# The down projection of a ConvFFN as seven block products over halves of tokens, channels and columns

## The chip, the cores and the metric

The kernel runs as one program on one core of a Trainium2 chip. The metric is the device time of one execution, in microseconds (us), from the first instruction of the program to its end. The kernel before the change has a median of 1789.0 us over three runs (1784.94 to 1791.03 us). Beside these there is one profiled execution, and the rows in this document come from it.

## The reference

One layer of a decoder step for 1024 prompt tokens and 64 sample tokens that share weights. Only the last part is touched here. After the attention branches the layer adds a ConvFFN, and after that comes the final norm:

```python
def conv_ffn(h, prefix, w_gate, w_up, conv_w, conv_b, w_down):
    L = h.shape[1]
    g = h @ w_gate
    u = h @ w_up
    ...
    f = (jax.nn.gelu(gc) * u) @ w_down
...
    x = x + f
...
y_prompt = rmsnorm(xp, final_norm_g)
```

Everything is float32. The down product is (tokens x 2816) @ (2816 x 1024). The inner width is D_FF = 2816 = 22 blocks of 128 channels.

## The kernel before, in words

A float32 product is made of three TensorE passes: each operand is split into a high part (a cast to fp32r on ACT, line 109) and a low part (source minus high part, on DVE, line 110), and high*high, high*low and low*high are summed in PSUM (`PASSES`, line 172). So every 128x1024 block that enters a product costs one ACT cast and one DVE subtraction. `split` is the helper that issues the two.

Lines 1169 to 1183 make the gate and up products. They run in 22 rounds of seven block products each (`products`), and the product gelu(gate)*up of a round is made on POOL (line 1182) and written to a DRAM tensor `f_d`, as 22 blocks of 128 channels x 1024 tokens (line 1183).

Line 1184 finishes the sample tokens' activations `fsv`: two small transposes on TensorE (`tr`, line 106), a multiply on DVE (line 1057) and the split into `fs` (line 1194).

Lines 1226 to 1266 are the down projection. Token tiles of 128 go in three groups of 3, 3 and 2. A group keeps two PSUM banks for each of its tiles, and walks over the 22 channel blocks: for each block it loads 128x1024 weights (`wr`, 512 KB, split into `wd`), for each pair of blocks the group's activations (`fr`, split into `fh`), and multiplies. A block with three tiles has 18 matmuls of 128x512. The sample tokens ride along in the second group: four matmuls per block (line 1258). The last group holds back its last four blocks and runs them tile by tile. `fin` (line 1203) adds the residual, sums squares on ACT, makes the reciprocal root (`rstd_of`, lines 112 to 123: six small DVE operations and one ACT root), scales on DVE and stores from SP's queue.

The order is that of a scheduler that keeps the program's dependencies and lays every engine's instructions in one row; each engine executes its row in order. All loads of this part are issued by SP, in order too. Raw weights and activations share a ring of four buffers (`raw`), split ones a ring of five (`hl`).

In the code after the change the same names hold. A "step" is one channel block of one block product, that is 12 matmuls (or 14 with the sample); `hd` is its split pair of operands.

Of the kernel before, what the change touches and what calls it, by code (L numbers as in the profile page):

```python
# [16 lines left out]
P = 128  # L17
# [15 lines left out]
def hybrid_step(ctx, tc, x_prompt, x_sample, mem_prompt, cache_k, cache_v, page_table, state_pool,  # L33
# [30 lines left out]
    ps = ctx.enter_context(tc.tile_pool(name="ps", bufs=1, space=bass.MemoryType.PSUM))  # L64
# [13 lines left out]
    def tpb():  # L78
        if tp2[0]:
# [5 lines left out]
    tp2 = [True, 0]  # L85

# [918 lines left out]
    with tc.tile_pool(name="fa", bufs=1, reuse_waits="tile") as fa:  # L1005
# [187 lines left out]
        fs = ap_.tile([P, NF, P], F32R, tag="act", bufs=4, name="fs")  # L1193
        split(fs[:, :, 0:TS], fs[:, :, TS:P], fsv)

    pB_cm.__exit__(None, None, None)
    with tc.tile_pool(name="fb", bufs=1, reuse_waits="tile") as fb:
        fr_b = [fb.tile([P, 2, 384], F32, name=f"fr{i}") for i in range(3)]
        fh_b = [fb.tile([P, 2, 2, 384], F32R, name=f"fh{i}") for i in range(3)]
        gfb = fb.tile([P, D], F32, name="gfb")  # L1200
        nc.sync.dma_start(gfb, bc(final_norm_g, P))

        def fin(t, banks, n, src, dst):
            xt = fb.tile([P, D], F32, tag="y", bufs=4, name=f"y{t}")[:n]
            nc.sync.dma_start(xt, src)
            ss2 = sm.tile([P, 2], F32, tag="ss2", name=f"ss{uid()}")[:n]
            for nb in range(2):
                xh = xt[:, nb * 512:(nb + 1) * 512]
                nc.vector.tensor_tensor(xh, xh, banks[nb][:n], op=ALU.add)
                if n < P:  # L1210
                    nc.vector.tensor_tensor(xh, xh, banks[nb][n:P], op=ALU.add)
                nc.scalar.activation(banks[nb][:n], xh, AF.Square, accum_out=ss2[:, nb:nb + 1])
            ss = sm.tile([P, 1], F32, tag="ss", name=f"ss{uid()}")[:n]
            nc.vector.tensor_tensor(ss, ss2[:, 0:1], ss2[:, 1:2], op=ALU.add)
            r = rstd_of(ss, n, 1.0 / D, 1)
            for nb in range(2):
# [109 lines left out]
```

## Time and profile before

| | |
|---|---|
| median of three runs | 1789.0 us |
| time of the profiled execution | 1788.88 us |
| its span, first to last instruction | 1787.1 us |
| mean granted TensorE clock | 0.987 of full speed |
| TensorE busy | 1724.8 us, 97% |
| DVE, ACT, POOL busy | 893.2, 724.4, 394.8 us |
| mean DMA rate | 131 GB/s |

The profiled execution lies 0.1 us from the median, and 1.8 us of it lie outside the span. A busy TensorE says only that matmuls were in its pipe; how fast they follow each other is read from the starts of groups in the timeline. The granted clock is a share of full speed: 1.00 is 2.4 GHz and 0.50 is 1.2 GHz.

### The profile page before, as it was taken

The page shows a single profiled execution, that of the slowest core. Times are in us where ns is not written, and L with a number is a line of the kernel's source. Part 1 is how long each engine was busy: PE and PEld are TensorE (multiplying, and loading weights), DVE is VectorE, ACT ScalarE, POOL GpSimd, SP SyncE. Part 2 cuts the span into 40 slices and gives each one's busy share as a digit, 9 for nine tenths or more (in the row PEclk, how much of TensorE's full clock was granted, in tenths as well). Part 3 has the DMA queues.
Part 4 walks back from the last instruction along what each step waited for, and adds up shares of the span by engine and source line. Part 5 has one row for each costly group of instructions (what it writes and reads, how often), then busy time and mean ns, then how long its engine had stood idle before and what let it go on. Part 6 is the DMA issues. An engine that isn't in the chain of part 4 may idle for free.

```text
span 1787.1 us, 23047 instructions
## 1 busy us (share of the span) xinstructions
PE 1724.8 (97%) x8289; PEld 1350.8 (76%) x8289; DVE 893.2 (50%) x1576; ACT 724.4 (41%) x1397; POOL 394.8 (22%) x428
## 2 busy tenths in 40 slices
PE   7999999998999999999989899999999999999997
PEld 5887876764666777767767688888888887888886
DVE  6411134230221666676725776666666666444365
ACT  5321235331221666665413344444444444333343
POOL 1113020301100324202201344444444441000000
PEclk9999999999999999999999999999999999999999
DMA  7432251367566334155442132222222224656454
GB/s 279 141 137 74 78 176 54 116 202 248 180 205 194 126 91 132 36 183 159 155 159 77 60 62 75 77 77 78 80 77 77 79 75 144 225 174 215 138 193 150
DMA packets 138600, 234.75 MB, mean 131 GB/s; under 512 B 25823, under 2 KB 71677, under 8 KB 138485
## 3 DMA queue, kind: packets, MB, share of 16 engines
q1 hardware_dynamic: 123349, 187.16, 32.8%
q0 software_dynamic: 15136, 46.12, 7.5%
q8 instruction: 65, 1.06, 0.2%
q14 instruction: 50, 0.41, 0.1%
HBM read 182.74 MB, written 50.54 MB: 131 GB/s over the span
## 4 chain that ended last, share of the span: by engine, by line
PE 86%; DVE 4%; DMA 3%; issue 2%; ACT 2%; SPq 1%; POOL 1%; DVEq 0%; POOLq 0%; ACTq 0%
PE nat L178 18%; PE big L1128 17%; PE big L1223 10%; PE nat L187 8%; PE nat L1128 7%; PE big L178 4%; PE tp L106 3%; PE nat L1223 3%; PE av L1043 3%; PE nat L195 2%; PE av L807 2%; PE big L777 2%; PE av L106 1%; PE av L567 1%; PE big L671 1%
## 5 line engine op out<-in xcount | busy, mean ns | idle before, releaser
L178 PE MATMUL nat<-act,hl 128*128 128x512 f32 x1344 | 359.1, 405 | 0.0
L178 PEld LDWEIGHTS nat<-act,hl 128*128 128x128 f32 x1344 | 242.7, 189 | 62.0 <-issue 15.1
L1223 PE MATMUL big<-wd,fh 128*128 128x512 f32 x792 | 189.7, 393 | 4.8 <-ACT fh L109 3.3
L187 PE MATMUL nat<-hl,act 128*128 128x512 f32 x768 | 186.5, 400 | 7.2 <-ACT nat L928 5.5
L1223 PEld LDWEIGHTS big<-wd,fh 128*128 128x128 f32 x792 | 149.7, 189 | 37.5 <-ACT fh L109 3.5
L187 PEld LDWEIGHTS nat<-hl,act 128*128 128x128 f32 x768 | 146.1, 192 | 39.2 <-ACT nat L928 6.0
L1128 PE MATMUL big<-B,wA 128*128 128x512 f32 x528 | 131.2, 396 | 0.0
L110 DVE TENSOR_TENSOR hl<-raw,hl 128x1024 fp32r<-128x1024 f32 x52 | 66.4, 1289 | 117.1 <-ACT hl L109 115.8
L110 DVE TENSOR_TENSOR wd<-wr,wd 128x1024 fp32r<-128x1024 f32 x66 | 82.7, 1254 | 80.4 <-ACT wd L109 80.3
L1128 PEld LDWEIGHTS big<-B,wA 128*128 128x128 f32 x528 | 95.9, 188 | 24.4 <-ACT gu L1153 6.3
L109 ACT CAST wd<-wr 128x1024 fp32r<-128x1024 f32 x66 | 69.5, 1053 | 89.2 <-PE tps L1258 41.9
L110 DVE TENSOR_TENSOR wB<-stm,wB 128x512 fp32r<-128x512 f32 x44 | 50.7, 1153 | 102.1 <-ACT wB L109 102.1
L470 POOL DMA_DIRECT2D gl<-ev x48 | 26.2, 546 | 280.4 <-ACT ev L469 256.1
L469 ACT COPY ev<-nat 128x512 f32<-128x512 f32 x48 | 28.1, 586 | 115.7 <-PE nat L178 115.2
L1128 PE MATMUL nat<-B,wC 128*128 128x512 f32 x264 | 70.5, 389 | 0.0
L1111 POOL TENSOR_TENSOR stm<-rf,stm 128x512 f32<-128x512 f32 x22 | 28.7, 1303 | 188.2 <-DVE wB L110 188.2
L109 ACT CAST hl<-raw 128x1024 fp32r<-128x1024 f32 x60 | 62.6, 1052 | 18.5 <-PE nat L178 7.8
L1223 PE MATMUL nat<-wd,fh 128*128 128x512 f32 x264 | 67.9, 392 | 0.0
L1128 PE MATMUL big<-T,wC 128*128 128x512 f32 x264 | 66.4, 400 | 0.0
L1128 PE MATMUL nat<-T,wB 128*128 128x512 f32 x264 | 64.9, 394 | 0.0
L1128 PE MATMUL big<-T,wD 128*128 128x512 f32 x264 | 64.0, 391 | 0.0
L1128 PE MATMUL big<-T,wB 128*128 128x512 f32 x264 | 63.4, 389 | 0.0
(434 smaller groups left out, 3106.4 us busy)
## 6 DMA issues: line engine op xcount, KB each, us to landing
wr<-in_w_ffn_down SPq DMA_DIRECT2D x66, 512.0 KB
raw<-in_w_in SPq DMA_DIRECT2D x40, 512.0 KB
kr<-in_cache_k SPq DMA_DIRECT2D x64, 256.0 KB
vr<-in_cache_v SPq DMA_DIRECT2D x64, 256.0 KB
gl<-ev POOLq DMA_DIRECT2D x48, 256.0 KB, 3.2
rf<-in_w_ffn_gate SPq DMA_DIRECT2D x22, 512.0 KB
rf<-in_w_ffn_up SPq DMA_DIRECT2D x22, 512.0 KB
f_d<-gu POOLq DMA_DIRECT2D x22, 512.0 KB, 4.0
```

Source lines behind the costliest of these rows:

```text
L106: nc.tensor.transpose(out, in_, ident[:n, :n])
L109: nc.scalar.copy(hi, src)
L110: (lo_eng or nc.vector).tensor_tensor(lo, src, hi.bitcast(F32), op=ALU.subtract)
L178: nc.tensor.matmul(out, wf(k, pw)[:, n0:n0 + P], acts[c][ph][:, k, :], start=(k == ks[0] and (pw, ph) == (0, 0)), stop=(k == ks[-1] and (p ...
L187: nc.tensor.matmul(out, acts[c][ph][:, k, o:o + P], wf(k, pw), start=(k == ks[0] and (pw, ph) == (0, 0)), stop=(k == ks[-1] and (pw, ph) = ...
L195: nc.tensor.matmul(out, stack[:, k, :], wf(k, pw), start=(k == ks[0] and pw == 0), stop=(k == ks[-1] and pw == 1))
L777: nc.tensor.matmul(S[:, k0:k0 + n], Qd[:, m, part, qs], Kst[:, m, k0:k0 + n], start=(part == 0), stop=(part == 1))
L807: nc.tensor.matmul(av[:, :P], aT[:, k * P:(k + 1) * P], vn[:, k0 + k], start=(k0 + k == 0), stop=(k0 + k == i))
L1043: nc.tensor.matmul(pt[:, i * 256:(i + 1) * 256].rearrange("p (h x) -> p h x", h=2), xs[:, k] if k < 4 else st2[:, k - 4], w[n1][:, :, k] i ...
L1111: nc.gpsimd.tensor_tensor(s4, a12, s2, op=ALU.subtract)
L1128: nc.tensor.matmul(out, wt[:, pw, k], Bt[:, ph, k], start=(start and k == 0 and (pw, ph) == (0, 0)), stop=(k == 3 and (pw, ph) == (1, 0)), ...
L1223: nc.tensor.matmul(bank, fh[:, ph, kk, i * P:(i + 1) * P], wh[:, pw, nb * 512:(nb + 1) * 512], start=(k == 0 and (pw, ph) == (0, 0)), stop ...
```

## The change

The product f (1024 tokens x 2816) times w_down (2816 x 1024) is cut into halves in all three directions: A11 to A22 (512 tokens x 1408 channels each) and B11 to B22 (1408 channels x 512 columns each). Instead of eight products of such blocks there are seven, on sums and differences of blocks (the scheme of Strassen in Winograd's form):

P1 = A11 B11, P2 = A12 B21, P5 = S1 T1 with S1 = A21+A22 and T1 = B11+B12, P6 = S2 T2 with S2 = S1-A11 and T2 = T1-B22, P7 = (A11-A21)(B12-B22), P3 = (A12-S2) B22, P4 = A22 (B21-T2).

They run in the order P1, P2, P5, P6, P7, P3, P4, eleven steps each, four PSUM banks at a time. P2 adds on to P1's banks and P7 to P6's. S1, T1 and then S2, T2 are kept in SBUF tiles `ST`, A11 and B22 in `XB`; the sums are made on DVE. The four output quarters are gathered in SBUF (`Y`, `U`), to which DVE and ACT bring each product from PSUM (`evac`). The sample's matmuls go along in P2, P6, P7 and P3, into one bank. Splits for the first four steps are issued inside the last round of the gate and up products (`first_down`); the sample's tail (line 1184 before) now stands behind those four steps. The norm of the first four token tiles and of the sample scales on ACT, multiplies by the gain on POOL and stores from POOL's queue; the last four tiles do it on DVE and SP as before.

```diff
+        ORDER = ("P1", "P2", "P5", "P6", "P7", "P3", "P4")
+        def prep_down(g):
+            p, k = steps[g]
+            if p == "P1":
+                if k < 4:
+                    src = rawt(fA(0, 0, k), wB(0, 0, k))
+                else:
+                    src = None
+                    ld(XB[k][:, 0], fA(0, 0, k))
+                    ld(ST[k][:, 1], wB(0, 0, k))
...
+            elif p in ("P5", "P6"):
+                src = ST[k]
+            elif p == "P7":
+                src = rawt(fA(1, 0, k), wB(0, 1, k))
+                tt(src[:, 0], XB[k][:, 0], src[:, 0], ALU.subtract)
+                tt(src[:, 1], src[:, 1], XB[k][:, 1], ALU.subtract)
...
+            h = pieces[g] = wp.tile([P, 2, 2, 512], F32R, tag="hl", bufs=5, name=f"hd{g}")
...
+                split(h[:, 0], h[:, 1], src)
+        def sum1(k):
+            ld(ST[k][:, 0], fA(1, 1, k))
+            if k < 4:
+                ld(ST[k][:, 1], wB(0, 0, k))
+            r = rawt(fA(1, 0, k), wB(0, 1, k))
+            tt(ST[k], ST[k], r, ALU.add)
+        def norm(x, i, dst, late):
...
+            r = rstd_of(ss, n, 1.0 / D, 1)
+            if late:
+                for c in (LO, HI):
+                    nc.vector.scalar_tensor_tensor(x[:, c], x[:, c], r, gfb[:n, c], op0=ALU.mult, op1=ALU.mult)
+                    nc.sync.dma_start(dst[:, c], x[:, c])
+            else:
+                nc.scalar.activation(x, x, AF.Identity, scale=r)
+                nc.gpsimd.tensor_tensor(x, x, gfb[:n], op=ALU.mult)
+                nc.gpsimd.dma_start(dst, x)
+        def smp2(c, op):
+            for h in range(2):
+                tt(ys[:, c], ys[:, c], sb[0][h * TS:(h + 1) * TS], op)
+        def evac(p, t, b):
+            y0, y1 = Y[t], Y[t + 4]
...
+            elif p == "P7":
+                tt(U[t], U[t], b, ALU.add)
+                tt(y1[:, HI], y1[:, HI], U[t], ALU.subtract)
+                sq(y1[:, HI], b, t + 4, 1)
+                tt(y1[:, LO], y1[:, LO], U[t], ALU.add)
+            elif p == "P3":
+                tt(y0[:, HI], y0[:, HI], b, ALU.add)
+                sq(y0[:, HI], b, t, 1)
+                norm(y0, t, y_prompt[t * P:(t + 1) * P], False)
+            else:
+                tt(y1[:, LO], y1[:, LO], b, ALU.add)
+                sq(y1[:, LO], b, t + 4, 0)
+                norm(y1, t + 4, y_prompt[(t + 4) * P:(t + 5) * P], True)
+        def run_steps(s0, s1):
...
+                if p == "P4" and k >= KH - 4:
+                    held.append((k, h))
+                    continue
+                for t in range(4):
+                    mm4(p, k, t, h)
+                if p in ("P2", "P6", "P7", "P3"):
...
+            if s1 == len(steps):
+                for t in range(4):
+                    for (k, h) in held:
+                        mm4("P4", k, t, h)
+                    evac("P4", t, banks[t])
...
+            nxt = prep(m + 1) if m + 1 < 2 * NG else first_down()
...
+        run_steps(0, 4)
         for g_ in late_s:
             for _ in g_:
                 pass
...
         split(fs[:, :, 0:TS], fs[:, :, TS:P], fsv)
+        nc.vector.tensor_tensor(fsv[:, 0:KH], fsv[:, 0:KH], fsv[:, KH:NF], op=ALU.add)
+        split(fs01[:, :, 0:TS], fs01[:, :, TS:P], fsv[:, 0:KH - 1])
...
-            for k2 in range(NF // 2):
-                nc.sync.dma_start(fr, f_d[2 * k2:2 * k2 + 2, :, c0:c0 + nt * P].rearrange("k p t -> p k t"))
-                split(fh[:, 0], fh[:, 1], fr)
...
-            for i, t in enumerate(ts):
-                for nb in range(2):
-                    for a in held:
-                        mm_down(banks[i][nb], i, nb, *a)
-                fin(t, banks[i], P, x1_d[t], y_prompt[t * P:(t + 1) * P])
+        run_steps(4, len(steps))
```

Up to the last round of the gate and up products every engine's row is the same in both kernels. Three places show what the rest of the text speaks of.

The first is DVE's row at the head of the down projection, before. `wd` and `fh` are split weights and activations, `fs` the split sample:

```order
L110 TENSOR_TENSOR wd_13553<-wr_13551,wd_13553 128x1024
L1057 TENSOR_TENSOR fsv<-fsv,tp_13446 128x128
L110 TENSOR_TENSOR fs<-fsv,fs 128x22x64
L110 TENSOR_TENSOR fh_13467<-fr_13464,fh_13467 128x768
L110 TENSOR_TENSOR wd_13579<-wr_13577,wd_13579 128x1024
```

The same place now. `hd_13450` belongs to the fourth step and `hd_13578` to the fifth; `sb_13526` is the bank of the sample's transposes:

```order
L114 TENSOR_TENSOR hd_13450<-rd_13447,hd_13450 128x1024
L1061 TENSOR_TENSOR fsv<-fsv,sb_13526 128x128
L114 TENSOR_TENSOR fsy<-fsv,fsy 128x22x64
L1411 TENSOR_TENSOR fsv<-fsv 128x704
L114 TENSOR_TENSOR fsy<-fsv,fsy 128x10x64
L114 TENSOR_TENSOR fsz<-fsv,fsz 128x64
L114 TENSOR_TENSOR hd_13578<-XB_13553,hd_13578 128x512
L114 TENSOR_TENSOR hd_13578<-ST_13554,hd_13578 128x512
```

The fifth step's splits stand behind the sample's multiply, and now behind two sample splits and a sum instead of one split.

On TensorE's row the sample's transposes stood ahead of the first down matmul:

```order
L1128 MATMUL big_13347<-T_9675,wD_13310 128x512 x12
L106 MATMUL tp_13446<-ident,gs_13331 128x64 x2
L106 MATMUL av_13450<-ident,gc 44x128
L1223 MATMUL big_13472<-wd_13481,fh_13467 128x512
L1223 MATMUL big_13473<-wd_13481,fh_13467 128x512
```

Now they stand behind the fourth step (the last row before them is that step's last bank):

```order
L1298 MATMUL P_13475<-hd_13450 128x512 x3
L1298 MATMUL P_13476<-hd_13450 128x512 x3
L1298 MATMUL P_13477<-hd_13450 128x512 x3
L110 MATMUL sb_13526<-ident,gs_13331 128x64 x2
L110 MATMUL sb_13530<-ident,gc 44x128
L1298 MATMUL P_13474<-hd_13578 128x512 x3
L1298 MATMUL P_13475<-hd_13578 128x512 x3
```

The transposes moved behind 48 matmuls of P1, and the fifth step's matmuls follow them.

The third place is POOL's row from the last round of the gate and up products to the end, before:

```order
L1182 TENSOR_TENSOR gu_13349<-gu_13349,gu_13336 128x1024
L1183 DMA f_d<-gu_13349 128x1024
L1182 TENSOR_TENSOR gu_13350<-gu_13350,gu_13342 128x1024
L1192 DMA out<-ncv 22x128
L1183 DMA f_d<-gu_13350 128x1024
```

The same place now, with the norms of four token tiles (`yy`) and of the sample (`uy`):

```order
L1387 DMA f_d<-gu_13350 128x1024
L1399 DMA out<-ncv 22x128 x2
L1263 TENSOR_TENSOR yy_13538<-yy_13538,uy 128x1024
L1264 DMA out<-yy_13538 128x1024
L1263 TENSOR_TENSOR uy<-uy 64x1024
L1264 DMA out<-uy 64x1024
L1263 TENSOR_TENSOR yy_13538<-yy_13538,uy 128x1024
L1264 DMA out<-yy_13538 128x1024
L1263 TENSOR_TENSOR yy_13538<-yy_13538,uy 128x1024 x2
L1264 DMA out<-yy_13538 128x1024 x2
```

POOL had no arithmetic in the down projection, and has five multiplies there now. On DVE's row the small operations of these five norms stand between the splits of P4's steps 3 to 10.

## Rows read from the trace of the kernel before

**Rows 1.** The page's busy times over the whole execution: busy us, share of the span, instructions.

```profile
PE 1724.8 (97%) x8289; PEld 1350.8 (76%) x8289; DVE 893.2 (50%) x1576; ACT 724.4 (41%) x1397; POOL 394.8 (22%) x428
PE 86%; DVE 4%; DMA 3%; issue 2%; ACT 2%; SPq 1%; POOL 1%; DVEq 0%; POOLq 0%; ACTq 0%
```

**Rows 2.** The table by stretch: busy us (and instructions) of each engine, granted clock, DMA share, GB/s. The stretch is the steady middle of the down projection.

```profile
1520.00:1705.00 185.00, 185.00 (x817) 152.96 (x817) 78.38 (x95) 64.60 (x78) 0.00 (x0) 1.00 0.56 184
```

**Rows 3.** TensorE's groups in the down projection: line, operation, count, busy us, mean ns, idle before them and what ended it.

```profile
L1223 PE MATMUL big<-wd,fh 128*128 128x512 f32 x792 | 189.7, 393 | 4.8 <-ACT fh L109 3.3 <-ACT big L1212 0.9 <-DVE fh L110 0.6
L1223 PE MATMUL nat<-wd,fh 128*128 128x512 f32 x264 | 67.9, 392 | 0.0
L1258 PE MATMUL tps<-wd,fs 128*128 128x512 f32 x44 | 13.5, 389 | 0.0
L1258 PE MATMUL av<-wd,fs 128*128 128x512 f32 x44 | 13.5, 389 | 0.0
```

**Rows 4.** The timeline of TensorE in the steady part: start, us, line, count.

```profile
1549.13 2.88 PE L1223 MATMUL big<-wd,fh 128*128 128x512 f32 x12
1551.85 1.52 PE L1223 MATMUL nat<-wd,fh 128*128 128x512 f32 x6
1553.21 2.88 PE L1223 MATMUL big<-wd,fh 128*128 128x512 f32 x12
```

**Rows 5.** The timeline of all engines where the down projection begins: start, us, engine, line, and in brackets the idle time before it and what ended it.

```profile
1508.83 0.34 PE L106 MATMUL tp<-ident,gs 64*128 64x64 f32 x2
1509.10 0.29 PE L106 MATMUL av<-ident,gc 128*44 128x128 f32 x1
...
1510.19 0.28 DVE L1057 TENSOR_TENSOR fsv<-fsv,tp 128x128 f32<-128x128 f32 x1
...
1510.50 1.36 ACT L109 CAST fs<-fsv 128x1408 fp32r<-128x1408 f32 x1 [0.82 <-DVE fsv L1057]
...
1512.65 0.81 PE L1223 MATMUL big<-wd,fh 128*128 128x512 f32 x2 [3.26 <-ACT fh L109]
...
1514.90 2.50 PE L1223 MATMUL big<-wd,fh 128*128 128x512 f32 x5 [0.59 <-DVE fh L110]
```

**Rows 6.** TensorE by stretch, first after the wait at 904 us and then after the one above: busy us (instructions), granted clock, DMA share, GB/s.

```profile
904.00:908.00 4.00, 0.52 (x3) 1.00 0.92 265
908.00:912.00 4.00, 1.95 (x5) 0.62 1.03 410
912.00:916.00 4.00, 4.00 (x11) 0.52 1.03 410
...
1512.00:1513.00 1.00, 0.35 (x2) 1.00 1.04 418
...
1519.00:1520.00 1.00, 1.00 (x4) 0.51 0.75 208
1520.00:1521.00 1.00, 1.00 (x5) 1.00 0.81 270
```

**Rows 7.** Groups of DVE and ACT in the down projection by shape: count, busy us, mean ns, idle before.

```profile
L110 DVE TENSOR_TENSOR wd<-wr,wd 128x1024 fp32r<-128x1024 f32 x61 | 74.7, 1224 | 74.3 <-ACT wd L109 74.2
L110 DVE TENSOR_TENSOR fh<-fr,fh 128x512 fp32r<-128x512 f32 x11 | 7.5, 686 | 5.6 <-ACT fh L109 5.6
L1209 DVE TENSOR_TENSOR y<-y,big 128x512 f32<-128x512 f32 x12 | 7.9, 684 | 7.4 <-PE big L1223 5.8 <-ACT big L1212 1.6
L119 DVE TENSOR_TENSOR rst<-rsy 128x1 f32<-128x1 f32 x8 | 1.1, 156 | 0.1
...
L109 ACT CAST wd<-wr 128x1024 fp32r<-128x1024 f32 x65 | 68.4, 1053 | 89.2 <-PE tps L1258 41.9 <-PE nat L1223 28.6 <-DMA wr<-in_w_ffn_down 6.5
L109 ACT CAST fh<-fr 128x512 fp32r<-128x512 f32 x11 | 6.9, 625 | 14.1 <-PE big L1223 14.1
```

**Rows 8.** DVE and POOL in the timeline where both work at once. The first two are two back-to-back 128x1024 splits on DVE beside one 128x512 addition on POOL, the next two one 128x512 split beside the 128x1024 multiply of line 1182, the last two an addition from PSUM beside a 128x512 operation on POOL.

```profile
843.77 3.46 DVE L110 TENSOR_TENSOR hl<-raw,hl 128x1024 fp32r<-128x1024 f32 x2
...
843.93 2.21 POOL L892 TENSOR_TENSOR g<-g,g 128x512 f32<-128x512 f32 x1 [5.28 <-DVE g L890]
...
1463.14 2.91 DVE L110 TENSOR_TENSOR wD<-rf,wD 128x512 fp32r<-128x512 f32 x1
...
1463.11 2.40 POOL L1182 TENSOR_TENSOR gu<-gu,gu 128x1024 f32<-128x1024 f32 x1 [0.75 <-DVE gu L1144]
...
1439.76 0.69 DVE L1144 TENSOR_TENSOR gu<-gu,big 128x512 f32<-128x512 f32 x1 [1.78 <-PE big L1128]
...
1439.09 1.28 POOL L1107 TENSOR_TENSOR stm<-rf 128x512 f32<-128x512 f32 x1
```

**Rows 9.** The table by stretch for the DMA rate (last two columns: share of 16 DMA engines, GB/s). The first stretch holds loads of 256 KB from the value cache; the second is a paced part of the down projection.

```profile
545.00:550.00 5.00, 5.00 (x26) 3.21 (x25) 0.00 (x0) 0.59 (x1) 0.54 (x1) 1.00 1.05 404
...
1580.00:1600.00 20.00, 20.00 (x90) 16.57 (x89) 7.84 (x8) 7.40 (x8) 0.00 (x0) 1.00 0.54 176
```

**Rows 10.** The end: TensorE's last group (its first matmul starts at 1754.74), the last tile's first addition, and its last scaling; and, from the timeline at 1717 us, the wait between the second and the third token group.

```profile
1754.74 22.60 PE L1223 MATMUL big<-wd,fh 128*128 128x512 f32 x99
...
1777.82 0.68 DVE L1209 TENSOR_TENSOR y<-y,big 128x512 f32<-128x512 f32 x1
...
1782.35 1.42 DVE L1218 SCALAR_TENSOR_TENSOR y<-y,rsy,gfb 128x512 f32<-128x512 f32 x2
...
1717.16 7.14 PE L1223 MATMUL big<-wd,fh 128*128 128x512 f32 x30 [0.91 <-ACT big L1212]
```

More of the change, by code (lines that the diff above doesn't have):

```diff
@@ L1167, in products, with fA, wB, ld @@
             return g0, g1
+        KH = NF // 2
+        ORDER = ("P1", "P2", "P5", "P6", "P7", "P3", "P4")
+        steps = [(p, k) for p in ORDER for k in range(KH)]
+        pieces, pend, held = {}, [], []
+        banks, sb = [], [None]
+        LO, HI = slice(0, 512), slice(512, D)
+        def fA(r, c, k):
+            return f_d[KH * c + k, :, r * 512:(r + 1) * 512]
+        def wB(r, c, k):
+            return w_ffn_down[(KH * r + k) * P:(KH * r + k + 1) * P, c * 512:(c + 1) * 512]
+        def ld(dst, src):
+            nc.sync.dma_start(dst, src)
@@ new lines, in rawt, with tt @@
+        def rawt(a, b):
+            r = wp.tile([P, 2, 512], F32, tag="raw", bufs=4, name=f"rd{uid()}")
+            for i, src in enumerate((a, b)):
+                if src is not None:
+                    ld(r[:, i], src)
+            return r
+        def tt(out, a, b, op):
+            nc.vector.tensor_tensor(out, a, b, op=op)
+        def prep_down(g):
[7 more added lines that the diff above has]
+                    ld(ST[k][:, 1], wB(0, 0, k))
+            elif p == "P2":
+                src = rawt(fA(0, 1, k), wB(1, 0, k))
+            elif p in ("P5", "P6"):
[5 more added lines that the diff above has]
+            elif p == "P3":
+                r = rawt(fA(0, 1, k), None)
+                src = XB[k]
+                tt(src[:, 0], r[:, 0], ST[k][:, 0], ALU.subtract)
+            else:
+                src = rawt(fA(1, 1, k), wB(1, 0, k))
+                tt(src[:, 1], src[:, 1], ST[k][:, 1], ALU.subtract)
+            h = pieces[g] = wp.tile([P, 2, 2, 512], F32R, tag="hl", bufs=5, name=f"hd{g}")
+            if src is None:
+                split(h[:, 0, 0], h[:, 1, 0], XB[k][:, 0])
+                split(h[:, 0, 1], h[:, 1, 1], ST[k][:, 1])
+            else:
+                split(h[:, 0], h[:, 1], src)
@@ L1169, in hybrid_step, with first_down @@
+        S1AT = {4 + (13 * k) // 10: k for k in range(KH)}
+        S2AT = {19 + (3 * k) // 2: k for k in range(KH)}
+        def first_down():
+            for g, n in ((0, 3), (1, 1), (2, 1), (3, 1)):
+                prep_down(g)
+                for _ in range(n):
+                    yield
         for _ in prep(0):
@@ L1194, in hybrid_step @@
+        Y = [ylo[t // 4][:, t % 4] for t in range(NT)]
+        uy = ap_.tile([P, 4096], F32, tag="act", bufs=4, name="uy")
+        U = [uy[:, t * 512:(t + 1) * 512] for t in range(4)]
+        ys = uy[0:TS, 2048:2048 + D]
+        gfb = uy[:, 2048 + D:]
         split(fs[:, :, 0:TS], fs[:, :, TS:P], fsv)
+        nc.vector.tensor_tensor(fsv[:, 0:KH], fsv[:, 0:KH], fsv[:, KH:NF], op=ALU.add)
+        split(fs01[:, :, 0:TS], fs01[:, :, TS:P], fsv[:, 0:KH - 1])
+        split(fsz[:, :, 0:TS], fsz[:, :, TS:P], fsv[:, KH - 1:KH])
```

160 lines of the change are left out of this document (99 added, 61 removed).

## The prediction

> **What bounds the kernel now.** I read the page's busy times and its chain first: TensorE is busy for 97% of the span, and 86% of the chain that ended last is TensorE [rows 1]. A mean over stages says little of one, so the table by stretch comes next: from 1520 to 1705 us TensorE is busy for all of 185 us at full clock, while DVE works for 78 us, ACT for 65 and POOL not at all [rows 2]. The down projection is thus bound by matmuls alone. Their number is 792 + 264 + 44 + 44 = 1144 [rows 3], and their pace is in the starts of the timeline: 18 in 1553.21 - 1549.13 = 4.08 us, 0.2267 us each [rows 4]. (The 393 ns of one are pipelined and are not its price.) 1144 of them are 259.3 us. The stage runs from the end of the last gate and up product, 1508.83 [rows 5], to 1754.74 + 22.60 = 1777.34 [rows 10], 268.5 us. Of the 9.2 us between, 0.6 are the transposes, 0.9 the wait between two token groups [rows 10], and the remaining 7.7 belong to the start: 3.26 and 0.59 us of waiting [rows 5], and what follows a wait: from 1513 to 1520 the granted clock is half [rows 6].
>
> The sum is made against the profiled execution, 1788.9 us, which is 0.1 below the median. A measurement of this kernel tells 0.3%, about 5.4 us, from no change.
>
> **Fewer matmuls.** Seven products of 11 steps with 12 matmuls are 924. The sample takes two in each step of four products: 88, as before. 1012 against 1144 are 132 fewer, of the same shape: 132 x 0.2267 = -29.9 us. The order's rows show that the work on TensorE's row is nothing else.
>
> **The start.** From here t counts from 1508.83. Steps 0 to 3 were split in advance, so the old wait goes and TensorE runs 48 matmuls to t = 10.9. Then come the transposes (to 11.45), and behind them on DVE's row the sample: the multiply 0.28, ACT's cast 1.36 [rows 5], a split of 1408, a sum of 704 and a split of 640 elements. By 1.22 us for 1024 and 0.69 for 512 [rows 7], DVE needs about 1.05 us per 1000 elements and 0.15 more: 1.6, 0.9 and 0.8. ACT's second cast and the small third split add 0.9. The fifth step's halves follow, two casts of 0.63 and two subtractions of 0.69, partly side by side. The chain ends near t = 18: TensorE waits 6.3 us instead of 3.85. Behind a wait of 5.5 us the clock was at half up to 916 us [rows 6]: 16 matmuls in 5.95 us instead of 3.6, 2.3 lost; at the old start 3.85 were. I take 3.0. Start: 9.3 against 7.7, +1.6. The old group change goes: -0.9.
>
> **Sums and differences.** Each step is one cast (1.05 us), one 1024-wide subtraction (1.22) and, in P1 and P2, ten sums of 1.22 in thirteen steps: 2.2 us of DVE in a step of 2.72 (3.17 with the sample). P7 needs two 512-wide differences more: 2.6 in 3.17. TensorE hides them as long as data are there; without that cover each step would cost the difference of DVE and TensorE. For the first sums, at the moment when no step is ready ahead, I take +1, between 0 and +8.
>
> **The sample's bank.** There is one bank for it. P7's first sample matmul needs P6's sums taken out, and P3's those of P7. At P6's end DVE has one split, four additions, one sample addition, a split and a second sample addition: about 6.8 us after the last step's begin, and TensorE arrives at 3.17 + 2.72 = 5.9: +1.0. At P7's end it has two splits and eight additions, first done at 8.9: +3.0, and I add 1 for the clock. Bounds for the two: 0 and 8.
>
> **The end of P4.** Five norms (four tiles and the sample) fall into it. I count from the begin of P3's last step. TensorE ends P4's seventh step at 3.17 + 7 x 2.72 = 22.2, then needs all four held pieces; the last low part is wanted at 22.2 + 9 x 0.2267 = 24.2. DVE must do until then: eight splits (9.8), five differences (3.4), six additions from PSUM (4.1), five chains of seven small operations of 0.16 (5.6): 22.9 us. That would fit. But POOL has five multiplies of 2.40 us now. The rows say what that does: a split of 0.69 that met the multiply of line 1182 took 2.91 and ended after it; two back-to-back splits of 1.22 took 3.46 with a POOL addition of 1.29 put between them; an addition from PSUM kept its 0.69 [rows 8]. So DVE's row becomes 22.9 + 12.0 = 34.9 us if every multiply stands in its way, 10.7 too long, and it fits if none does. Following the row (ACT's scaling of a tile waits for DVE's root, POOL for ACT, DVE's next split for POOL), I find each multiply but the last directly in the way of a split and the last low part near 33: +8.5. TensorE stands nearly still for it, so the clock falls again: +2.5. Sum +11, bounds 0 and 14.
>
> The Trainium skill, page "SBUF — State Buffer", section "Who interferes with whom", calls this an exclusive lock: a DVE instruction with two SBUF inputs and a GpSimd instruction that reads SBUF block each other, whichever starts first. The trace agrees (2.91 us for 0.69). By the rule alone DVE might keep the lock through a run of splits, and the term would be 0; the row with 3.46 us shows POOL getting in between two.
>
> **The tail.** After the last matmul come 9.8 us now (1777.34 to 1787.1): addition, root, scaling to 1783.8 [rows 10], store. Four tiles follow each other every 2.72 us instead of two every 5.44, but with one addition each; DVE needs about 3.6 us per tile (0.7 + 1.4 and seven of 0.16, with ACT's answers between) and is late by 3 at the last. I take 0, between -1 and +3.
>
> Sum: 1788.9 - 29.9 + 1.6 - 0.9 + 1 + 1 + 4 + 11 + 0 = **1776.7 us**, a gain of 12 out of 30.
>
> **Rivals.** First, the covers hold: POOL's multiplies fall beside ACT's casts and additions from PSUM, and the sample's bank is free in time. Then 15 us of the sum go: 1762, with its neighbours 1757 to 1768. For it speaks that DVE is busy for 42% of the stretch [rows 2]; against it, that POOL got in between two back-to-back splits [rows 8]. Chance 0.2.
>
> Second, no change that can be told: the locks take their upper bound (+14), the sums theirs (+8) and each new wait brings half clock. 1776.7 + 3 + 7 = 1787, between 1784 and 1794. Against it: two bounds must be met together. Chance 0.16.
>
> Third, slower: the loads of P1 and P2. Most of SP's loads are 256 KB now instead of 512, and in SP's row 46 of them (12.1 MB) stand between the one that reuses the memory of the sample's activations (free at t = 17) and the last one of P2. TensorE reaches P2's last step at t = 11.45 + 9.3 + 7 x 2.72 + 10 x 3.17 = 71.5, and splitting takes 2.3 of it: 52 us, 233 GB/s. Loads of 256 KB ran at 404 GB/s with DMA engines full; the paced part of the down projection had 176 [rows 9]. At 176 the last piece comes 17 us late, and waits with half clock cost some more: 1794 to 1800. The rival decides below 174 GB/s; if the ring of four raw buffers holds the queue at such a rate, the gain is gone. Against it: each buffer is held for some 6 us, four of them give 4 x 0.52 MB in 6 us, 350 GB/s. Chance 0.07.
>
> The Trainium skill, page "DMA: Bandwidth & Descriptors", section "Bandwidth", speaks for this rival: batch transfers to 1 MiB or more for 75% of the peak, with 138 GB/s measured at 64 KB and 341 at 1 MB. An estimate of mine half way between the page's two figures, 240 GB/s, would only just do. The trace disagrees: 404 GB/s with 256 KB each.
>
> **How the numbers follow.** My forecast has 0.57, and holds 1768 to 1783.5. With the first rival (0.2), faster by more than 0.3%, that is below 1783.6, has 0.77; within 0.3% 0.16; slower 0.07. The range leaves out the lower half of the first rival and the third rival with the upper part of the second: 1761 to 1788.
>
> **What would show it.** In the new profile: 1012 matmuls in the down projection at 4.08 us per 18; one wait of about 6 us behind the 48th, ended by ACT's cast, and half clock after it; a wait of 1 us at P7's and 3 us at P3's first sample matmul, released by DVE; and in P4's held part splits of 1.22 that last 2.5 to 3.6 beside POOL's multiplies, with TensorE waiting 8 us in sum. It is wrong if TensorE waits for raw loads in P2, if the held part runs without a wait, or if the stage between 1508.8 and the last matmul is not near 256 us.

## The result and the profile after

The changed kernel takes 1770.3 us in the median of four runs (1768.7 to 1770.7), the kernel before, beside it on the same chip, 1787.0. The ratio is 0.990 (95% interval 0.9885 to 0.9916), about 1% faster; the medians are 16.7 us apart. The forecast was 1776.7.

The profiled execution took 1768.7 us, its span is 1767.0. The page's busy times and its chain by engine, the rows that answer to [rows 1]:

```profile
PE 1698.4 (96%) x8157; PEld 1327.8 (75%) x8157; DVE 952.8 (54%) x1648; ACT 723.2 (41%) x1397; POOL 412.1 (23%) x438
PE 84%; DVE 6%; DMA 3%; issue 3%; ACT 2%; SPq 1%; POOL 1%; DVEq 0%; POOLq 0%; ACTq 0%
```

There are 8289 - 8157 = 132 fewer matmuls on TensorE (PE), as the change says. DVE has 60 us more work, and the chain goes through DVE for 6% of the span instead of 4%.

TensorE's groups in the down projection (answer to [rows 3]; the stretch begins at 1508 us, three matmuls late):

```profile
L1298 PE MATMUL P<-hd 128*128 128x512 f32 x921 | 222.9, 397 | 12.9 <-ACT hd L113 6.1 <-DVE hd L114 4.5 <-ACT P L1250 2.3
```

Instead of 4.8 us TensorE now waits 12.9, and for three kinds of work: ACT's casts, DVE's low parts, and ACT's square (line 1250), which stands in no term of the forecast. Where that is, the timeline of TensorE shows (start, us, count, and in brackets the wait before it and what ended it; answer to [rows 5] and [rows 10]):

```profile
1507.06 11.34 PE L1298 MATMUL P<-hd 128*128 128x512 f32 x48
1518.33 0.34 PE L110 MATMUL sb<-ident,gs 64*128 64x64 f32 x2
1519.14 0.27 PE L110 MATMUL sb<-ident,gc 128*44 128x128 f32 x1 [0.47 <-DVE fsv L1061]
1524.97 23.81 PE L1298 MATMUL P<-hd 128*128 128x512 f32 x96 [5.57 <-ACT hd L113]
1548.62 0.61 PE L1338 MATMUL sb<-hd,fsy 128*128 128x512 f32 x2
1549.07 2.88 PE L1298 MATMUL P<-hd 128*128 128x512 f32 x12
...
1552.24 2.88 PE L1298 MATMUL P<-hd 128*128 128x512 f32 x12
...
1680.60 2.43 PE L1298 MATMUL P<-hd 128*128 128x512 f32 x10
1685.34 6.86 PE L1298 MATMUL P<-hd 128*128 128x512 f32 x22 [2.32 <-ACT P L1250]
...
1719.69 20.11 PE L1298 MATMUL P<-hd 128*128 128x512 f32 x88
1739.97 0.73 PE L1298 MATMUL P<-hd 128*128 128x512 f32 x2 [0.17 <-DVE hd L114]
1741.20 0.50 PE L1298 MATMUL P<-hd 128*128 128x512 f32 x1 [0.50 <-ACT hd L113]
1746.04 11.64 PE L1298 MATMUL P<-hd 128*128 128x512 f32 x41 [4.34 <-DVE hd L114]
```

Fourteen matmuls from 1549.07 to 1552.24 take 3.17 us, 0.2267 each: the pace of [rows 4]. The stage lasts from 1507.06 to 1746.04 + 11.64 = 1757.68, 250.6 us instead of 268.5. I cut it at three places, and the same cuts serve for the experiments: A to P2's first sample matmul (1548.62), B to P3's first matmul (1680.60), C to P4's first (1719.69), D to the end.

| | matmuls alone | forecast | measured |
|---|---|---|---|
| A: start and P1 | 144 x 0.2267 = 32.6 | + 0.6 + 9.3 = 42.5 | 41.6 |
| B: P2 to P7 | 582: 131.9 | + 1 + 1 = 133.9 | 132.0 |
| C: P3 | 154: 34.9 | + 3 + 1 = 38.9 | 39.1 |
| D: P4 | 132: 29.9 | + 11 = 40.9 | 38.0 |
| sum | 229.4 | 256.2 | 250.6 |

B is more than half of the stage and runs at the matmuls' pace to 0.1 us. What is lost stands in A, C and D, and part of it is no wait. The table by stretch (columns as in [rows 6], granted clock third from the right) behind the three waits, and in B:

```profile
1525.00:1528.00 3.00, 3.00 (x7) 2.17 (x8) 3.00 (x6) 2.93 (x6) 0.00 (x0) 0.50 1.05 389
...
1685.00:1689.00 4.00, 3.66 (x9) 2.88 (x10) 3.94 (x7) 0.40 (x3) 0.00 (x0) 0.57 0.00 0
...
1746.00:1750.00 4.00, 3.96 (x9) 3.11 (x10) 1.80 (x2) 0.70 (x2) 0.00 (x0) 0.50 0.66 262
...
1550.00:1680.00 130.00, 130.00 (x575) 107.61 (x574) 104.57 (x117) 50.79 (x56) 0.00 (x0) 1.00 0.55 191
```

After each of these three waits the granted clock is at or near half for 3 to 4 us and more: 96 matmuls from 1524.97 to 1548.62 take 23.65 instead of 21.76 us, 1.9 lost, and the last 41 take 11.64 instead of 9.3. In B DVE works for 104.6 of 130 us, 80%, and it hides.

### The profile page after: what moved, and what is told of

Same layout as the page of the kernel before. It is cut to its first block, busy times and chain, and to the rows that moved or that the text cites. A ratio compares the mean times of both kernels' runs of the same rounds, so it can differ in the third digit from the quotient of the medians.

```text
span 1767.0 us, 22904 instructions
## 1 busy us (share of the span) xinstructions
PE 1698.4 (96%) x8157; PEld 1327.8 (75%) x8157; DVE 952.8 (54%) x1648; ACT 723.2 (41%) x1397; POOL 412.1 (23%) x438
## 4 chain that ended last, share of the span: by engine, by line
PE 84%; DVE 6%; DMA 3%; issue 3%; ACT 2%; SPq 1%; POOL 1%; DVEq 0%; POOLq 0%; ACTq 0%
PE nat L182 18%; PE big L1132 17%; PE P L1298 10%; PE nat L191 8%; PE nat L1132 7%; PE big L182 4%; PE tp L110 4%; PE av L1047 3%; PE big L781 2%; PE av L811 2%; PE nat L199 2%; PE av L110 1%; PE av L571 1%; PE sb L1338 1%; PE big L675 1%
## 5 line engine op out<-in xcount | busy, mean ns | idle before, releaser
L1298 PE MATMUL P<-hd 128*128 128x512 f32 x924 | 223.7, 397 | 12.9 <-ACT hd L113 6.1
L1298 PEld LDWEIGHTS P<-hd 128*128 128x128 f32 x924 | 176.7, 192 | 52.5 <-ACT hd L113 6.7
L114 DVE TENSOR_TENSOR hd<-rd,hd 128x1024 fp32r<-128x1024 f32 x37 | 49.3, 1334 | 30.2 <-ACT hd L113 25.9
L113 ACT CAST hd<-rd 128x1024 fp32r<-128x1024 f32 x37 | 38.9, 1051 | 60.1 <-PE sb L1338 31.9
L1148 DVE TENSOR_TENSOR gu<-gu,big 128x512 f32<-128x512 f32 x44 | 30.3, 688 | 57.2 <-PE big L1132 57.2
```

What stands on the lines that cost most here:

```text
L113: nc.scalar.copy(hi, src)
L114: (lo_eng or nc.vector).tensor_tensor(lo, src, hi.bitcast(F32), op=ALU.subtract)
L1148: nc.vector.tensor_tensor(hv(g, i), hv(g, i), q(x), op=ALU.add)
L1298: nc.tensor.matmul(banks[t], h[:, ph, 0, t * P:(t + 1) * P], h[:, pw, 1], start=(k == 0 and p not in ("P2", "P7") and (pw, ph) == (0, 0)), ...
```

## Experiments

All ratios are to the kernel before, on the same chip as the run; the changed kernel's is 0.990 (0.9885 to 0.9916). The gate and up products end at 1507 to 1511.5 us in the profiled executions, a spread that stands ahead of every edit, so the stretches A to D are the finer measure; each of them is read from one profiled execution.

### The end of P4: POOL's multiplies (e1, e2)

```diff
-                nc.gpsimd.tensor_tensor(x, x, gfb[:n], op=ALU.mult)
```

> Leaves out the multiplication by the final gain for the token tiles 0 to 3 and for the sample (POOL's five instructions at the end); their outputs lack the gain, all else is as in the changed kernel. Theory (POOL's multiplies block DVE's two-input instructions, about 2.1 us each, and DVE's row is 19 us without them, within the 24 that TensorE gives): the 128x1 operations of line 126 last 0.15 us again instead of 2.2, the waits of TensorE on the low parts in P4's held part (0.17 + 0.50 + 4.34 us) go, and with them some 2 us of half clock: 1762 to 1765 us. Rival (the five chains of small operations between DVE and ACT are by themselves too long for the stretch): a wait of 3 us or more on the last low part stays, 1768 to 1771 us.

1765.5 us, ratio 0.986 (0.984 to 0.989). P4 is one row without a wait in TensorE's timeline:

```profile
1725.70 30.08 PE L1297 MATMUL P<-hd 128*128 128x512 f32 x132
```

D is 30.1 us instead of 38.0: the five multiplies cost 7.9, and the rival has fallen. One execution each would be thin evidence, but every kernel of this document agrees: D is 37.6 to 38.6 in the eight that keep POOL's multiplies and 30.1 to 30.6 in the five without them. (C was 41.3 here, 2.2 worse, so the whole time gains less.) DVE's groups by shape in the same stretch show where the lock fell, first of the changed kernel, then of e1:

```profile
L114 DVE TENSOR_TENSOR hd<-rd,hd 128x1024 fp32r<-128x1024 f32 x8 | 11.8, 1484 | 0.0
L1197 DVE TENSOR_TENSOR rd<-rd,ST 128x512 f32<-128x512 f32 x6 | 6.3, 1045 | 0.4 <-DMA rd<-in_w_ffn_down 0.4
...
L126 DVE TENSOR_TENSOR rsy<-rsy,rst 128x1 f32<-128x1 f32 x6 | 5.2, 862 | 0.1
...
L126 DVE TENSOR_TENSOR rsy<-rsy,rst 64x1 f32<-64x1 f32 x1 | 2.2, 2160 | 0.0
```

```profile
L114 DVE TENSOR_TENSOR hd<-rd,hd 128x1024 fp32r<-128x1024 f32 x8 | 9.7, 1220 | 0.7 <-ACT hd L113 0.7
...
L1197 DVE TENSOR_TENSOR rd<-rd,ST 128x512 f32<-128x512 f32 x6 | 4.1, 684 | 3.2 <-DMA rd<-in_w_ffn_down 3.2
L126 DVE TENSOR_TENSOR rsy<-rsy,rst 128x1 f32<-128x1 f32 x6 | 0.9, 157 | 0.1
...
L126 DVE TENSOR_TENSOR rsy<-rsy,rst 64x1 f32<-64x1 f32 x1 | 0.1, 144 | 0.0
```

The splits cost 2.1 us more beside POOL, the differences 2.2, the 128x1 products of line 126 4.3 and the sample's 2.1: 10.7 in sum, one stall of about 2.1 for each multiply. Three of the five stalls hit an operation of one element per partition, 0.15 us long. One of these and the last two in the timeline of the changed kernel, on DVE:

```profile
1727.20 2.16 DVE L126 TENSOR_TENSOR rsy<-rsy,rst 64x1 f32<-64x1 f32 x1
...
1739.83 2.86 DVE L1197 TENSOR_TENSOR rd<-rd,ST 128x512 f32<-128x512 f32 x1
1742.62 4.50 DVE L114 TENSOR_TENSOR hd<-rd,hd 128x1024 fp32r<-128x1024 f32 x2
```

and on POOL at the same time:

```profile
1739.26 5.64 POOL L1263 TENSOR_TENSOR yy<-yy,uy 128x1024 f32<-128x1024 f32 x2 [0.45 <-ACT yy L1262]
```

The difference, 0.69 us of work, ends at 1742.69, behind POOL's first multiply; the first of two splits is then held until the second multiply is done, at 1744.90 (TensorE, which waits for it, goes on at 1746.04), and the pair takes 4.50 us instead of 2.36 in e1.

Can DVE do the five gains itself?

```diff
-                norm(y0, t, y_prompt[t * P:(t + 1) * P], False)
+                norm(y0, t, y_prompt[t * P:(t + 1) * P], True)
...
-                    norm(ys, NT, y_sample, False)
+                    norm(ys, NT, y_sample, True)
```

> All nine norms scale and multiply by the gain on DVE in one pass (two 128x512 instructions of 0.70 us, stored by SP), so POOL's five multiplies and ACT's five scalings go and DVE gets ten instructions more. Theory (the lock is the price): DVE gives back five stalls of about 2.05 us (10.3) and takes ten starts of about 0.62 us (6.2), its row is about 25.5 us against 24.2 that TensorE gives, so a wait of 0 to 1.5 us is left of 5.0, with little half clock: 1763 to 1767 us. Rival (DVE is simply too full there, whoever multiplies): the wait on the last low part stays at 4 us or more, 1769 to 1773 us.

1766.7 us, ratio 0.987 (0.984 to 0.990). D is 30.6 us, with no wait on a low part at all, where up to 1.5 us were expected:

```profile
1725.31 30.64 PE L1298 MATMUL P<-hd 128*128 128x512 f32 x132
```

Ten instructions more on DVE (with five scalings fewer on ACT) are cheaper than five on POOL that block it.

### The start: the sample's tail and the loads (e3, e5, e6)

```diff
-        ps_cm.__exit__(None, None, None)
-        pq.append(ctx.enter_context(tc.tile_pool(name="pq", bufs=1, space=bass.MemoryType.PSUM, reuse_waits="tile")))
-        run_steps(0, 4)
         for g_ in late_s:
...
         split(fsz[:, :, 0:TS], fsz[:, :, TS:P], fsv[:, KH - 1:KH])
+        ps_cm.__exit__(None, None, None)
+        pq.append(ctx.enter_context(tc.tile_pool(name="pq", bufs=1, space=bass.MemoryType.PSUM, reuse_waits="tile")))
+        run_steps(0, 4)
```

> The sample's tail (its two transposes, the multiply on DVE, the transposes of the conv state and the splits of the sample's operand) stands in the program ahead of P1's first four steps instead of behind them. Theory (the 5.57 + 0.47 us of waiting behind the 48th matmul are the sample's chain and nothing else): its 7 us of DVE and ACT run beside the 48 matmuls (10.9 us), piece 4 is split in time, the wait goes and with it about 1.5 us lost at half clock: 1761 to 1764 us, stage 243 us. Rival (the memory of the sample's activations, or DVE's and ACT's backlog behind the last gate and up products, decides): TensorE waits 3 us or more ahead of P1 or at P1's fifth step, 1767 to 1772 us.

1772.3 us, ratio 0.991 (0.988 to 0.993): nothing gained. A is 41.4 us against 41.6 (from the transposes, which come first here). The rival held, but with the loads in place of its two causes. TensorE, ACT and SP in the timeline of e3:

```profile
1526.22 14.07 PE L1298 MATMUL P<-hd 128*128 128x512 f32 x49 [4.78 <-ACT hd L113]
```

```profile
1524.87 0.62 ACT L113 CAST hd<-XB 128x512 fp32r<-128x512 f32 x1 [8.50 <-DMA XB<-f_d]
```

```profile
1512.11 2.07 SPq L1187 DMA_DIRECT2D yy<-x_d  x4
...
1516.12 0.87 SPq L1187 DMA_DIRECT2D XB<-f_d  x1
```

The sample's chain is done by 1517.2, but ACT stands idle for 8.5 us, for the fifth step's load. SP issues it behind 1.75 MB that are needed only later (rows of x1 and the gain), which the scheduler had moved ahead. So two chains of nearly equal length, the sample's and the load's, end at the fifth step, and taking away one shows the other. The next two kernels give the fifth and sixth step raw buffers, whose loads go out early, with and without the moved tail:

```diff
-                if k < 4:
+                if k < 6:
                     src = rawt(fA(0, 0, k), wB(0, 0, k))
```

> The sample's tail ahead of P1 as in e3, and the pieces of P1's fifth and sixth step come through the raw buffers, like the four ahead of them, instead of through XB and ST (their four 256 KB halves are loaded once more for the sums). Theory (what held e3's fifth step was no longer the sample's chain but the loads of XB and ST, which SP issues behind the 1.75 MB for the outputs): steps 4 and 5 are split in time, the next loads have 5.4 us more, the wait at the fifth step goes and at most 2 us of it come back at the seventh: the first 10 steps of P1 within 29 us of the last gate and up product, 1762 to 1766 us. Rival (ACT and DVE are the ones that are late there, whatever the loads do): 4 us or more of waiting stay at the fifth or sixth step, 1769 to 1773 us.

> The raw buffers for P1's fifth and sixth step alone; the sample's tail stays behind P1's first four steps. Theory (in the changed kernel the wait is the sample's chain of 6.6 us from its transposes, and it may be covered by any two steps that are split ahead of it): the fifth and sixth step run without a wait, the chain ends 1.5 to 2.5 us behind them and TensorE waits so long at the seventh step, instead of 5.6 at the fifth: 1764 to 1768 us. Rival (the wait is the loads, as in e3, and the sample's chain stands only beside them): a wait of 4 us or more at the seventh step, released by ACT's cast of a piece that has just landed, 1769 to 1773 us.

e5: 1765.1 us, ratio 0.987 (0.985 to 0.988), A = 36.4. e6: 1766.0 us, 0.987 (0.985 to 0.989), A = 36.8. Both gain 5 us there. In e6 the wait is 2.58 us, at the seventh step:

```profile
1521.11 5.04 PE L1298 MATMUL P<-hd 128*128 128x512 f32 x21
1528.73 16.93 PE L1298 MATMUL P<-hd 128*128 128x512 f32 x72 [2.58 <-ACT hd L113]
```

Its length is what e6's theory said (1.5 to 2.5 us), but for the last 1.7 us before its cast of that piece ACT waited for a load, not for the sample's chain: both theories own a part. In e5 0.28 us are left at the seventh step, and 1.23 us come up at P2's first matmuls, for ACT's copies of P1's banks.

### Between P7 and P3 (e4, e7, e8, e10)

The forecast had 3 us here, for the sample's one bank. The trace shows 2.32, but at a product's matmul, ended by ACT's square. The square of P7's first tile writes over that tile's bank, and with seven banks P3's fourth tile gets the same one.

```diff
-                sq(y1[:, HI], b, t + 4, 1)
                 tt(y1[:, LO], y1[:, LO], U[t], ALU.add)
+                sq(y1[:, HI], U[t], t + 4, 1)
```

> P7's squares write their unused elementwise result over U[t] (SBUF, no longer needed there) behind the last addition from it, instead of over the PSUM bank of the product. Theory (the 2.32 us wait between P7 and P3 is the ring of seven banks: P3's fourth tile needs the bank of P7's first tile, held until ACT's square has read its turn): the bank is free after DVE's addition, the wait falls to 0.3 us or less and the half clock behind it goes, 2 to 4 us: 1766 to 1768 us. Rival (the sample's one bank, as forecast, is as late): a wait of 2 to 3 us comes back at P3's first sample matmul, released by ACT or DVE reading that bank, 1769 to 1771 us.

1771.7 us, ratio 0.990 (0.987 to 0.992), C = 38.9 against 39.1: a miss. The wait is still 1.91 us and now ended by DVE's addition from the bank. So the square was the last link only; the addition was late already. e7 puts it ahead in the program:

```diff
+                last7 = p == "P7" and k == KH - 1
+                if s + 4 < len(steps) and s0 > 0 and not last7:
                     prep_down(s + 4)
...
+                if last7:
+                    prep_down(s + 4)
```

> e4's edit, and in P7's last step the taking out of P7's first tile stands ahead of the two differences and the split for four steps later. Theory (the wait between P7 and P3 is one of DVE's order: the bank that P3's fourth tile takes waits for DVE's addition, which stood behind two differences and a split, 2.4 us, and then for ACT's square): the addition starts when TensorE has done the tile, the wait at P3's fourth tile (2.3 us, 1.9 in e4) goes: 1766 to 1768 us, the stage 2 to 4 us shorter. Rival (DVE's whole row at P7's end, eight additions and four for the sample, is too long, and the sample's bank comes next): a wait of 2 us or more stands at P3's first sample matmul or at its fifth to seventh matmul group, 1769 to 1771 us.

1771.3 us, ratio 0.990 (0.989 to 0.992), C = 38.6. The rival held:

```profile
1685.17 4.87 PE L1298 MATMUL P<-hd 128*128 128x512 f32 x20 [0.36 <-DVE uy L1197]
1692.70 1.19 PE L1339 MATMUL sb<-hd,fsy 128*128 128x512 f32 x4 [2.66 <-ACT sb L1250]
```

Here is the wait of the forecast: the sample's bank, 2.66 us. In the changed kernel it was hidden behind the other. e8, which keeps e4's and e7's idea, frees that bank early as well.

```diff
+                if last7:
+                    tt(U[0], U[0], banks[0], ALU.add)
+                    smp2(LO, ALU.subtract)
+                    smp2(HI, ALU.add)
+                    sq(ys[:, LO], XB[10][0:TS, 0], NT, 0)
+                    prep_down(s + 4)
```

> In P7's last step DVE takes the first tile's bank and then the sample's four additions, ahead of the differences and the split for later steps and of the other three tiles; the squares of P7 and of the sample's first half write their unused result to SBUF (U, XB) instead of the banks. Theory (two waits stand one behind the other at P7's end, the bank of the first tile and then the sample's one bank, both by the order of DVE's and ACT's work): neither is left above 0.3 us at P3's first three steps, the clock stays at its upper level there, the stage is 3 to 4.5 us shorter than the changed kernel's 250.6: 1765 to 1767 us. Rival (DVE's row is too full there in any order): a wait of 1.5 us or more stands at one of P3's first five steps, released by DVE, 1768 to 1771 us.

1773.1 us, ratio 0.992 (0.989 to 0.994), C = 39.7, a wait of 2.81 at the sample's matmul: a miss. DVE's timeline at P7's end, in the changed kernel and in e8:

```profile
1678.09 0.69 DVE L1197 TENSOR_TENSOR rd<-rd,ST 128x512 f32<-128x512 f32 x1 [2.19 <-DMA rd<-in_w_ffn_down]
...
1682.65 0.69 DVE L1197 TENSOR_TENSOR uy<-uy,P 128x512 f32<-128x512 f32 x1
```

```profile
1681.13 0.69 DVE L1197 TENSOR_TENSOR rd<-rd,ST 128x512 f32<-128x512 f32 x1 [3.49 <-DMA rd<-in_w_ffn_down]
...
1684.48 0.69 DVE L1197 TENSOR_TENSOR uy<-uy,P 128x512 f32<-128x512 f32 x1
```

DVE is not too full; it stands idle for 2.2 and 3.5 us, in front of a difference of the form `rd<-rd,ST` with a piece of w_down. That is P4's, whose first step is twelve steps away: the scheduler had moved it ahead of P7's sums, and the engine keeps its row. P3's differences go to `XB` and let go of the raw buffers at once, so nothing held P4's back. e10, on top of e8's edit, keeps P3's in the raw buffers until they are split:

```diff
                 r = rawt(fA(0, 1, k), None)
-                src = XB[k]
-                tt(src[:, 0], r[:, 0], ST[k][:, 0], ALU.subtract)
+                src = None
+                tt(r[:, 0], r[:, 0], ST[k][:, 0], ALU.subtract)
```

> e8's order at P7's end, and P3's differences stay in the raw buffer (each is split there, as two halves, as P1's are) instead of going to XB, so that at most four of them and none of P4's can be ahead on DVE's row. Theory (what made DVE late at P7's end were the differences of P3 and P4 that the scheduler had moved ahead of P7's sums: DVE stood in its row for their loads, 2.2 us in the changed kernel, 3.5 in e8): DVE takes the first tile's bank within 1 us of its last matmul, no wait above 0.5 us is left between P7's last step and P3's fourth, the upper clock stays, the stage is 3 to 4.5 us shorter than the changed kernel's 250.6: 1765 to 1767 us. Rival (DVE has simply too much to do there, 12 sums of 0.6 us, 4 splits and 4 differences in 13 us): a wait of 1.5 us or more stays at P3's first sample matmul, 1769 to 1772 us.

1766.8 us, ratio 0.987 (0.986 to 0.989), C = 35.3 against 34.9 for its matmuls alone; no wait of TensorE is left between 1526 and 1737 us. DVE takes the bank at 1680.63, while P7's last step (from 1679.01) still runs:

```profile
1680.63 0.69 DVE L1197 TENSOR_TENSOR uy<-uy,P 128x512 f32<-128x512 f32 x1
```

C shows it twice: 35.3 in both kernels with this edit (e10, e11), 37.0 to 41.3 in the eleven without. Whether the edit would do without e8's order was not run.

### Together (e9, e11)

e9_all and e9_all6 join e2's edit, e8's, and `k < 7` or `k < 6` for the raw buffers; e11 adds e10's.

> Three edits together: the gains on DVE (e2), the raw buffers for the first seven pieces of P1 (e6 had six), and e8's order at P7's end. Theory (the three places are apart and their gains add): 4.1 from P4 (e2's stage against the changed kernel's), 5.5 to 8 from the start (e6's 5.5, and its wait of 2.6 us covered by one more step), 3 to 4.5 from P7's end: a stage of 234 to 238 us, 1753 to 1758 us, faster than the changed kernel by 0.7 to 1.0%. Rival (what goes at one place comes back at the next, as in e3 and e7: DVE, busy for 34 of 40 us in P2, has no room for an earlier TensorE): waits of 3 us or more in P2 to P6, where there are none now, 1760 to 1765 us.

> As e9_all with the raw buffers for six pieces as in e6. Theory (gains add): the wait of 2.6 us at P1's seventh step stays, stage 236 to 240 us, 1755 to 1760 us, 1 to 4 us behind e9_all. Rival (the seventh piece through the raw buffers costs more loading than its step covers): no slower than e9_all.

> e9_all (gains on DVE, seven pieces of P1 through the raw buffers, the order at P7's end) with e10's differences in the raw buffer. Theory: as e9_all, whose wait of 2.0 us and half clock at P7's end go: 3 to 5 us below e9_all's 1761.0, 1755 to 1759 us. Rival (in e9_all the wait stays, DVE being full): 1760 to 1763 us.

e9_all: 1761.0 us, ratio 0.985 (0.983 to 0.987), a stage of 243.6; e9_all6: 1764.3 us, 0.986 (0.984 to 0.989), 240.4. Neither is in its range, the stages are longer than the 234 to 238 and 236 to 240 us expected, and the intervals of the two overlap. P4 gave its 7.4 us in both, and C gave little (38.8 and 38.4 against 39.1), as in e8. In e9_all the start had gained nothing (A and B together 174.3 us against 173.5): a wait of 2.90 us at the eighth step brought half clock for nearly 7 us, and a wait of 1.56 us stood in P2, ended by ACT's cast of a piece whose load had just landed. The rival's time holds, with late loads in the place of a full DVE. e11: **1758.7 us, ratio 0.982 (0.981 to 0.984)**, a stage of 235.3, faster than the kernel before and, by the intervals, than the changed one. TensorE's waits in it, and its P4:

```profile
PE P L1299 <- ACT hd L113: 2.3, 4, 1.0
```

```profile
1714.52 30.63 PE L1299 MATMUL P<-hd 128*128 128x512 f32 x132
```

Of the 21 us that the changed kernel's stage lost beside its matmuls, 6 are left: 2.3 of waits in P1 and P2, all ended by ACT's casts, 0.6 of transposes, 0.7 in P4, 0.4 in P3, and 1.9 in small gaps.

## Why the prediction was right, and where not

**The gain** of 1.0% was forecast as 0.7%, in its range, by the mechanism named. *Fewer matmuls* came out exactly: 132 fewer at 0.2267.

**The start** was right in kind: a wait of 5.57 + 0.47 us behind the 48th matmul (6.3 forecast), ended by ACT's cast, and half clock worth 1.9 (3.0). What the step didn't see is the load of the same piece: in e3 its cast could begin 15.5 us after the last gate and up product, when it had landed; in the changed kernel, behind the sample's chain, it began 16.7 after it (1523.79). SP's row had been read for the rate up to P2's end, not for what stands ahead of the first load to XB.

**Sums and differences** cost 0 where +1 was taken: TensorE waits for none of them from 1548.62 to 1680.60.

**The sample's bank.** Its term was +1.0 and +4; B shows 0 for the first, C 4.2 for the second. That the second size is right is luck: the reason is one that the step did not have. It took the program's order for the engine's. TensorE's row after the change, from P3's begin:

```
L1298 MATMUL P_14717<-hd_14621 128x512 x3
L1298 MATMUL P_14718<-hd_14621 128x512 x3
L1298 MATMUL P_14719<-hd_14621 128x512 x3
L1298 MATMUL P_14717<-hd_14641 128x512
L1298 MATMUL P_14720<-hd_14621 128x512 x3
...
L1298 MATMUL P_14719<-hd_14661 128x512 x2
L1338 MATMUL sb_14721<-hd_14621,fsy 128x512 x2
L1338 MATMUL sb_14721<-hd_14641,fsy 128x512 x2
```

The scheduler had put the first two steps' sample matmuls into the third step, behind 32 matmuls instead of 12, so the sample's bank could be 4.5 us later than reckoned; the fourth product bank P_14720, which no step of the forecast counted, came first. And DVE was late because of P4's differences in its row (e8, e10), not because of the two splits and eight additions that the step counted. The first term, at P7's begin, came to 0 by the same scheduler. TensorE there, and then DVE:

```profile
1645.63 4.25 PE L1298 MATMUL P<-hd 128*128 128x512 f32 x18
1649.72 0.63 PE L1338 MATMUL sb<-hd,fsy 128*128 128x512 f32 x2
```

```profile
1648.71 0.69 DVE L1197 TENSOR_TENSOR uy<-uy,sb 64x512 f32<-64x512 f32 x1
```

DVE was done with the sample's bank at 1649.40, 6.9 us behind the begin of P6's last step (1642.46), as forecast (6.8). In the program's order, behind 12 matmuls, TensorE would have come at 1648.35 and waited the 1.0 us of the term; behind 18 it came at 1649.72.

**The end of P4** was the right mechanism, mis-sized: +11 forecast, 8.1 measured (D less its matmuls), of which 7.9 vanish with the multiplies (e1). Each multiply did stand in the way, though three of them in that of an operation of 0.15 us and not of a split: 10.7 us of stalls against 12.0. The error is in the 22.9 us for DVE's own row. It adds durations, but back-to-back instructions overlap: a split of 1.22 us begins 1.14 before the next instruction, an operation of 0.15 takes 0.07 of the row (up to 0.19 if the next one needs its result). Three rows of DVE in the changed kernel:

```profile
1718.00 1.22 DVE L114 TENSOR_TENSOR hd<-rd,hd 128x1024 fp32r<-128x1024 f32 x1
1719.14 0.15 DVE L1197 TENSOR_TENSOR ss<-ssf 128x1 f32<-128x1 f32 x1
1719.21 0.68 DVE L1197 TENSOR_TENSOR yy<-yy,P 128x512 f32<-128x512 f32 x1
```

By starts the row is 8 x 1.14 + 11 x 0.61 + 35 x 0.1 = 19.3, with the stalls 30.0, and the last low part was ready at 1742.62 + 4.50 = 1747.12, 30.6 after the begin of P3's last step (1716.52); the forecast had 33. TensorE stood still for the low part before it, the third held piece's, and went on at 1746.04: waits of 0.17 + 0.50 + 4.34 = 5.0 us instead of 8.5, and 2.3 of half clock instead of 2.5. The first rival, that the covers hold, falls with the 7.9 us of e1, and the second, that no change can be told, with the interval of the ratio.

The Trainium skill, page "SBUF — State Buffer", section "Who interferes with whom", gave the rule for this term, that a DVE instruction with two SBUF inputs and a GpSimd one that reads SBUF block each other; the trace agrees down to an operation of 64x1, 2.16 us instead of 0.14.

**The tail** is 1767.0 - 1757.68 = 9.3 us instead of 9.8. **The third rival** (loads of P1 and P2 below 174 GB/s) fell: TensorE waits for none in P2. But its place is the next limit: e11's DMA engines are full from 1540 to 1590.

```profile
1540.00:1590.00 50.00, 48.62 (x211) 38.78 (x210) 35.79 (x33) 21.51 (x26) 0.00 (x0) 1.00 1.00 356
```

The Trainium skill, page "DMA: Bandwidth & Descriptors", section "Bandwidth", would have given about 240 GB/s by my estimate; the trace has 356 with loads of 256 KB, so the measurement decides.

Of the 8.0 us between the forecast and the profiled execution (1776.7 and 1768.7), 5.6 are the stage's; 1.8 lie ahead of it, where no term stands (its first matmul came at 1507.06 instead of 1508.83, and in the experiments at up to 1511.5), and the tail makes the rest.

## What to carry to other kernels

A count of steps in the program is not the order on an engine: read each engine's row around every bank and buffer that changes hands, and ask of each row what an instruction that was moved ahead waits for, since all behind it wait too. Two chains that end together hide each other, so an edit that takes away one alone shows no gain (e3, e4, e7) and proves nothing against the theory until the next wait has been read. Give elementwise work that runs beside DVE's two-input operations to DVE itself if DVE's row has the time: ten instructions of 0.74 us there were 7 us cheaper than five on POOL.

## What was not expected of the hardware

A wait of 2 to 3 us sometimes costs the clock and sometimes not. After waits of 2.58 us (e6), 2.66 (e7) and 2.82 (e9_all6, at 1691) the granted clock stays at 1.00; after 1.91 (e4), 1.98 (e9_all), 2.32 (the changed kernel) and 2.81 (e8) it falls to half for over 3 us, and after 2.90 and 3.23 (e2 and e1, at P3) for nearly 7. Two waits of the same length at the same matmul, 2.81 us in e8 and 2.82 in e9_all6, and the second microsecond behind each, first e8:

```profile
1692.53:1693.53 1.00, 1.00 (x4) 0.81 (x3) 1.00 (x3) 0.73 (x1) 0.00 (x0) 0.50 0.00 0
```

```profile
1692.47:1693.47 1.00, 1.00 (x6) 0.84 (x5) 1.00 (x3) 1.00 (x2) 0.00 (x0) 1.00 0.00 0
```

So a short wait's price has a part that no reckoning here foresaw, from nothing up to 2.9 us (the same 36 matmuls of P1 took 11.36 us behind the 2.90 us in e9_all and 8.48 behind 0.96 in e11), as much as the wait itself. What decides it stays open; it wasn't tried.
